# A transformer layer on one core: a new plan of the instruction order, with corrected durations and leads

## The chip, the cores and the metric

The kernel runs on 1 core of a Trainium2 chip. The metric is the time of one execution on the device in microseconds (us); it is given as the median of several runs. The engines of the core are TensorE (PE in the profile), VectorE (DVE), ScalarE (ACT), GpSimd (POOL) and SyncE (SP), which here only issues transfers. Each engine works through its own instructions in the order in which they are issued, and waits where an operand isn't there yet.

## What is computed

One layer of a transformer, in float32, for one sequence of 1024 tokens of width 1024. The mixer has sixteen groups of 64 columns from four kinds of mixing: NSA attention (compressed, selected and windowed keys with gates), a short convolution, stick-breaking attention, and dilated attention. The reference, cut to its frame:

```python
def hybrid_layer(x, ...):
    hn = rms_norm(x, g_mix)
    proj = hn @ w_in                      # split into the columns of the four mixers
    o_a = nsa_mixer(qa, ...)              # 4 heads
    o_b = short_conv_mixer(cvb, cvc, cvu, conv_w)
    o_c = stick_breaking_attention(qc, kc, vc)        # 4 heads
    # q and k of the dilated heads are normed; three dilations, mixed by a softmax over their lse
    o_d = jnp.sum(mix_w[..., None] * jnp.stack(outs, axis=0), axis=0)
    groups = rms_norm(groups, g_out.reshape(N_GROUPS, HEAD_DIM)).reshape(b, s, MIX_WIDTH)
    x = x + groups @ w_out
    h2 = rms_norm(x, g_ffn)
    return x + (jax.nn.silu(h2 @ w_gate) * (h2 @ w_up)) @ w_down      # d_ff = 2816
```

## The kernel before

**Products.** A float32 product is made as three products of a faster type on PE (`mm3`, L240 to L243): each operand is split into a high part (a copy, mostly by ACT, L107) and a low part (the difference, by POOL or DVE, L108), and high·high, high·low and low·high are summed in PSUM. Tiles are named by what they hold, with a number when they are told apart: `PRp`, `Tp`, `SPp` and `Op` are PSUM banks of four kinds, `S` scores, `pth`/`ptl` transposed probabilities in two parts, `MO` a block of the mixer's output (64 channels of two heads by 256 tokens), `whi`/`wlo` and `fw` split weights, `raw`/`fraw` weights as loaded.

**Stages.** First the input's norm, projections and the compressed keys. Then the mixers in the order `n0 c0 n1 c1 ps0 s0 ps1 s1 pd0 d0 pd1 g d1`: n are NSA heads by pairs (`attn_nsa`, L626), c the convolution (`conv`, L798), ps and pd the projections of stick-breaking and dilated heads (`proj_stick`, `proj_dil`), s and d their attention, and g the gains of the grouped norm (`gains`). Last the output projection with residual (`out_half`, L893), the second norm, and the feed-forward part: gate and up as Winograd's seven products per 2x2 of blocks (`winograd`, L1036; its additions are all at L1033), the products of down likewise. The projections of the values are transposed: ACT copies the product to `vraw` (L367), PE transposes it in four (L370), ACT and DVE split it into `VD` or `VC` (L373, L374). The dilated heads' queries and keys go through L311/L312 (`dqh`, `dql`, on 64 partitions) and L319 to L321 (`dkh`, `dkl`, `dkr`; a transfer at L320 copies each to the other 64 partitions). Outputs of a block of attention leave PSUM by an ACT copy `otmp` (L580) and a DVE add on 64 partitions (L582). `finish` (L592) norms a block: squares, a product with a block matrix of ones (L608), Ln and Exp on ACT (L609, L610), a DVE multiply, and a store of `MO` to the DRAM tile `mixd` (L617; the last one by `flush_stores`, L621). `gains` loads the seven rows of `mixd` back as `gm` (L836, 512 KB each); `gain` scales each by the norm's weight into the high part `MH` (L817 on POOL for one half of the tokens, L819 on ACT for the other) and the low part `ML` (L820, DVE). The eighth row stays in SBUF. In NSA, L549 subtracts distances and takes the minimum (`mm`) of a block of scores; L651 scales the probabilities by `ll`, L685 multiplies queries with compressed keys.

**The order.** What the program text says is not the order of issue. The program is recorded once; `_traced` (L1912) finds each instruction's dependences, gives it a duration by a formula (`_duration`, L1849) and a lead: `EARLIER` by kind plus `LEADS` by group, which is engine, pool tag and tile name, plus `LEADS` by group and stage (`@10`, the number of marks passed; 6 is s0, 10 is d0, 12 is g, 13 is d1, 15 gate/up). `_planned` (L1972) then runs a model of the five engines: of the instructions whose operands are there, each engine takes the one with the smallest number less its lead; tiles get slots when they are first written; a transfer takes a fixed time and a time for its bytes. `fix_order` (L2135) makes each engine issue in order of the planned starts, up to the first instruction that uses the pool `f2`: the products of down run in program order. The second recording gets the same slots.

## Time and profile before

| | us |
|---|---|
| median of 3 runs | 1306.11 |
| lowest, highest | 1305.69, 1307.82 |
| the profiled execution's own time | 1303.94 |
| its span, first to last instruction | 1302.1 |
| PE busy | 1276.2 |
| DVE busy | 977.5 |
| ACT busy | 701.9 |
| POOL busy | 654.5 |
| mean granted clock of PE, share of full speed | 0.997 |

All times of rows come from the one profiled execution, and count from the start of its span. An engine's busy time divided by the span says how full it is, the idle time of the fullest one where time is lost. The list of waits names, for each place where PE stood still, what released it; the timeline shows the instructions of an engine in order with their starts.

### The profile page before, as it was taken

How to read it: one execution, taken by the hardware profiler on the slowest of the kernel's cores; microseconds unless marked ns; L12 is line 12 of the kernel's file. 1: busy time of each engine (PE TensorE's matmuls, PEld its weight loads, DVE VectorE, ACT ScalarE, POOL GpSimd, SP SyncE). 2: the span in 40 equal slices, each digit the busy share in tenths (PEclk: the TensorE clock that was granted, in tenths of full speed). 3: DMA queues.
4: the chain of work that ended last, by engine and by line, in shares of the span. 5: the costliest groups of instructions: out<-in, count | busy, mean ns of one | idle time of the engine just before them, and what ended most of it. 6: DMA issues, size and time to landing. Idle time of an engine off the chain costs nothing.

```text
span 1302.1 us, 20263 instructions
## 1 busy us (share of the span) xinstructions
PE 1276.2 (98%) x7041; PEld 1086.6 (83%) x7041; DVE 977.5 (75%) x1793; ACT 701.9 (54%) x1437; POOL 654.5 (50%) x490
## 2 busy tenths in 40 slices
PE   8999999999999999999999999999999999999998
PEld 7988888888888898899987888878888787887886
DVE  5858888888898888962577788676776667499962
ACT  6567678678888877653654332332333335523540
...
GB/s 250 97 125 6 9 91 24 18 82 56 46 48 25 94 68 138 173 107 162 188 175 121 186 154 178 94 86 121 120 91 81 98 113 345 265 199 73 145 98 153
DMA packets 90550, 153.04 MB, mean 118 GB/s; under 512 B 10128, under 2 KB 35728, under 8 KB 90448
## 3 DMA queue, kind: packets, MB, share of 16 engines
...
q0 software_dynamic: 560, 1.84, 0.4%
...
q14 instruction: 47, 0.39, 0.1%
...
## 4 chain that ended last, share of the span: by engine, by line
PE 85%; DVE 7%; DMA 2%; ACT 2%; issue 2%; POOL 1%; SPq 0%; DVEq 0%; POOLq 0%; ACTq 0%
PE PRp L241 11%; PE PRp L243 10%; PE PRp L242 10%; PE Tp L570 4%; PE PRp L1056 4%; PE PRp L1054 4%; PE PRp L1055 4%; PE SPp L522 3%; PE SPp L1056 2%; PE Tp L1056 2%; PE SPp L1054 2%; PE Tp L1054 2%; PE SPp L1055 2%; PE Tp L1055 2%; PE Op L575 2%; PE SPp L524 2%
## 5 line engine op out<-in xcount | busy, mean ns | idle before, releaser
L108 POOL TENSOR_TENSOR wlo<-raw,whi 128x512 fp32r<-128x512 f32 x94 | 129.4, 1385 | 84.9 <-ACT whi L107 56.2
L1043 POOL TENSOR_TENSOR fw<-fraw,fw 128x512 fp32r<-128x512 f32 x50 | 72.5, 1449 | 131.7 <-ACT fw L1042 118.9
L559 DVE TENSOR_TENSOR ptl<-Tp,pth 128x512 fp32r<-128x512 f32 (+2 forms) x172 | 102.2, 605 | 20.2 <-ACT pth L558 17.9
L1114 DVE TENSOR_TENSOR fw<-sraw,fw 128x512 fp32r<-128x512 f32 x73 | 91.6, 1273 | 33.1 <-ACT fw L1113 32.7
L558 ACT ACTIVATE pth<-Tp 128x512 fp32r<-128x512 f32 (+2 forms) x172 | 90.3, 531 | 44.0 <-PE Tp L570 15.0
L1042 ACT ACTIVATE fw<-fs 128x512 fp32r<-128x512 f32 x88 | 52.6, 628 | 105.1 <-DVE fs L1033 77.2
L1114 POOL TENSOR_TENSOR hw<-bB,hw 128x512 fp32r<-128x512 f32 x55 | 81.0, 1486 | 47.8 <-ACT hw L1113 47.1
L570 PE MATMUL Tp<-ident,S 128*128 128x128 f32 x552 | 94.0, 275 | 1.2 <-DVE S L651 0.7
L241 PE MATMUL PRp<-XH,whi 128*128 128x512 f32 x224 | 91.3, 408 | 0.9 <-ACT raw L357 0.9
L242 PE MATMUL PRp<-XL,whi 128*128 128x512 f32 x224 | 90.3, 403 | 0.0
L243 PE MATMUL PRp<-XH,wlo 128*128 128x512 f32 x224 | 90.0, 403 | 0.0
L107 ACT ACTIVATE whi<-raw 128x512 fp32r<-128x512 f32 x102 | 63.0, 620 | 46.4 <-PE PRp L242 19.5
L1043 DVE TENSOR_TENSOR fw<-fs,fw 128x512 fp32r<-128x512 f32 x88 | 71.9, 846 | 14.8 <-ACT fw L1042 14.7
L651 POOL TENSOR_SCALAR S<-S,ll 128x640 f32<-128x640 f32 (+7 forms) x32 | 53.6, 1675 | 54.1 <-DVE ll L649 19.3
L570 PEld LDWEIGHTS Tp<-ident,S 128*128 128x128 f32 x552 | 67.7, 141 | 11.5 <-DVE ptl L559 1.4
L243 PE MATMUL PRp<-whi,ML 128*128 128x256 f32 (+1 forms) x248 | 71.0, 289 | 1.0 <-DVE ML L820 1.0
L1033 POOL TENSOR_TENSOR u<-u,p 128x512 f32<-128x512 f32 x22 | 32.2, 1462 | 78.9 <-DVE u L1033 40.8
L793 POOL TENSOR_TENSOR S<-S,R 128x128 f32<-128x128 f32 (+7 forms) x32 | 45.7, 1430 | 51.0 <-DVE R L791 49.3
L241 PE MATMUL PRp<-whi,MH 128*128 128x256 f32 (+1 forms) x248 | 70.7, 288 | 0.4 <-DVE x L903 0.4
L242 PE MATMUL PRp<-wlo,MH 128*128 128x256 f32 (+1 forms) x248 | 70.9, 287 | 0.0
L1042 ACT ACTIVATE fw<-fraw 128x512 fp32r<-128x512 f32 x50 | 31.4, 627 | 69.9 <-PE Tp L1056 18.1
L1113 ACT ACTIVATE hw<-bB 128x512 fp32r<-128x512 f32 x62 | 38.9, 628 | 53.1 <-PE Op L243 21.5
...
## 6 DMA issues: line engine op xcount, KB each, us to landing
...
```

Source lines behind the costliest of these rows:

```text
L108: (lo or nc.gpsimd).tensor_tensor(dst_lo, raw, f(dst_hi), op=OP.subtract)
L241: nc.tensor.matmul(ps, a[0], b[0], start=first, stop=False)
L242: nc.tensor.matmul(ps, a[0], b[1], start=False, stop=False)
L243: nc.tensor.matmul(ps, a[1], b[0], start=False, stop=last)
L558: nc.scalar.activation(ph[:, c], tp[:, :n], AF.Copy)
L559: nc.vector.tensor_tensor(pl[:, c], tp[:, :n], f(ph[:, c]), op=OP.subtract)
L570: nc.tensor.transpose(tp[:, i * 128:(i + 1) * 128], p, ident)
L1043: eng.tensor_tensor(wt[:, 1, :], a, f(wt[:, 0, :]), op=OP.subtract)
L1054: nc.tensor.matmul(ps, wt[:, 0, c], bh[:, k, :], start=k == 0, stop=False)
L1055: nc.tensor.matmul(ps, wt[:, 0, c], bl[:, k, :], start=False, stop=False)
L1056: nc.tensor.matmul(ps, wt[:, 1, c], bh[:, k, :], start=False, stop=k == 3)
L1114: eng.tensor_tensor(wt[:, 1, :], raw, f(wt[:, 0, :]), op=OP.subtract)
```

## The change

Three things, all in the planning; no instruction is added or taken away, and no operand changes. First, durations: narrow fp32r products on PE get a floor of 110 ns instead of 56 (times 0.92), except where the next one has the same stationary operand; ACT and DVE instructions on at most 64 partitions get 115 ns more; the constants of ACT, DVE and POOL rise by some 7 to 35 ns. Second, the table `LEADS` is new as a whole: 523 entries for 563, 356 of them for one stage (358 before). Third, `REUSES` names two more pools.

```diff
-REUSES = {"bp": ("sm",), "lp": ("sm",)}
+REUSES = {"bp": ("sm",), "lp": ("sm",), "lq": ("sm",), "b2": ("lq",)}
...
 LEADS = {
...
-    "ACT otmp tk @10": -205,
...
-    "DVE whl u": -1153,
-    "DVE whl u @15": -17,
...
+    "ACT otmp tk @10": -4858,
...
+    "DVE whl u": 3741,
+    "DVE whl u @15": -1289,
...
     if eng == "PE":
         if "float32r" in str(i.ins[1].dtype):
-            return max(56, n * 35 / 32 / 2.4) * PE_RATE
+            return max(110, n * 35 / 32 / 2.4) * PE_RATE
...
+    extra = 115 * (outs[0].ap[0][1] <= 64 and n > 1)
     if eng == "ACT":
-        return n / 1.2 + (51 if psum else 93) + 93 * small
+        return n / 1.2 + (66 if psum else 103) + 93 * small + extra
...
-            return 2.13 * n + 62 + 61 * (small > 0)
+            return 2.13 * n + 69 + 61 * (small > 0)
         if ty == "InstTensorCopy" and not psum:
-            return .52 * n + 69
+            return .52 * n + 77 + extra
         if ty == "InstTensorScalarPtr" and len(big) == 1 and not psum:
-            return .52 * n + 69 + 61 * small
-        return 1.04 * n + 69 + 61 * (max(0, small - 1) if ty == "InstCustomDveAnt" else small)
+            return .52 * n + 77 + 61 * small
+        return 1.04 * n + 78 + extra + 61 * (max(0, small - 1) if ty == "InstCustomDveAnt" else small)
     if ty == "InstDMACopy":
         return 1000
     if ty == "InstTensorScalarPtr":
-        return 2.5 * n + 260
+        return 2.5 * n + 280
...
-    return 165 * n + 300 if "pow" in str(i) else 2.1 * n + 150
+    return 165 * n + 300 if "pow" in str(i) else 2.1 * n + 185
...
-    ops, history, first, tags, bare = [], {}, {}, {}, {}
+    ops, history, first, tags, bare, last = [], {}, {}, {}, {}, None
...
+        if op.eng == "PE" and "float32r" in str(i.ins[1].dtype) and acc[0].n < 240:
+            w = str(i.ins[1].bass_ap)
+            narrow, last = (ops[last[1]] if last and last[0] == w else None), (w, op.n)
+            if narrow:
+                narrow.dur = acc[0].n * 35 / 32 / 2.4 * PE_RATE
+        elif op.eng == "PE":
+            last = None
```

Three places in the order that comes out. The first is DVE at the end of gate/up (1080 us of the profile before): `u2`, `u3` and `p5` are running sums of the seven products, PRp_12198 is the product with T4, PRp_12179 that with B22, Op_12140 that with B21, and `fw` the low parts of split weights for down. Before, DVE has:

```order
L1114 TENSOR_TENSOR fw_12250<-fraw_12248,fw_12250 128x512
L1114 TENSOR_TENSOR fw_12254<-fraw_12248,fw_12254 128x512
L1033 TENSOR_TENSOR u2_12101<-PRp_12179,u2_12101 128x512
L1114 TENSOR_TENSOR fw_12259<-fraw_12257,fw_12259 128x512
L1033 TENSOR_TENSOR u2_11960<-u2_12101,u2_11960 128x512
L1033 TENSOR_TENSOR p5_11994<-p5_12135,p5_11994 128x512
L1033 TENSOR_TENSOR u3_12156<-PRp_12198,u3_12156 128x512
L1033 TENSOR_TENSOR u3_12015<-u3_12156,u3_12015 128x512
L1033 TENSOR_TENSOR s2_12218<-s1_12216,p1_11938 128x512
L1114 TENSOR_TENSOR fw_12263<-fraw_12257,fw_12263 128x512
```

and in the changed kernel:

```order
L1114 TENSOR_TENSOR fw_12250<-fraw_12248,fw_12250 128x512
L1033 TENSOR_TENSOR u2_12101<-PRp_12179,u2_12101 128x512
L1114 TENSOR_TENSOR fw_12254<-fraw_12248,fw_12254 128x512
L1033 TENSOR_TENSOR u2_11960<-u2_12101,u2_11960 128x512
L1114 TENSOR_TENSOR fw_12259<-fraw_12257,fw_12259 128x512
L1033 TENSOR_TENSOR p5_11994<-p5_12135,p5_11994 128x512
L1033 TENSOR_TENSOR p1_12079<-Op_12140,p1_12079 128x512
L1033 TENSOR_TENSOR u3_12156<-PRp_12198,u3_12156 128x512
L1033 TENSOR_TENSOR p1_11938<-p1_12079,p1_11938 128x512
L1114 TENSOR_TENSOR fw_12263<-fraw_12257,fw_12263 128x512
L1033 TENSOR_TENSOR u3_12015<-u3_12156,u3_12015 128x512
```

The sum `p1` with the product Op_12140, which stood further ahead, now lies between `p5` and the sum with PRp_12198. On PE the product PRp_12198 stands 12 matmuls earlier, and Op_12140 is the last one; from there to the matmul that takes the bank of PRp_12198 again there are seven.

The second is DVE in the first NSA stage (160 us). S_1918 are the probabilities of one block, ll_1917 its sums; MO_1735 the output of the block before; Sc0_782 compressed scores. Before:

```order
L549 ISA S_1984,mm_1981<-SPp_1986,W_1303,mm_1981 128x256
L549 ISA mm_1981 128x1
L549 ISA S_1984,mm_1981<-SPp_1996,W_1303,mm_1981 128x256
L549 ISA mm_1981 128x1
L582 TENSOR_TENSOR MO_1735<-Op_1736,otmp_1886 64x128
L559 TENSOR_TENSOR ptl_1911<-Tp_1907,pth_1910 128x256
L582 TENSOR_TENSOR MO_1735<-Op_1736,otmp_1886 64x128
L549 ISA Sc0_782,mm_2065<-SPp_2063,wct_1306 128x63
L549 ISA mm_2065 128x1
L651 TENSOR_SCALAR S_1918<-S_1918,ll_1917 128x768
```

and in the changed kernel:

```order
L549 ISA S_1984,mm_1981<-SPp_1986,W_1303,mm_1981 128x256
L549 ISA mm_1981 128x1
L559 TENSOR_TENSOR ptl_1881<-Tp_1877,pth_1880 128x256
L549 ISA S_1984,mm_1981<-SPp_1996,W_1303,mm_1981 128x256
L549 ISA mm_1981 128x1
L549 ISA Sc0_782,mm_2065<-SPp_2063,wct_1306 128x63
L549 ISA mm_2065 128x1
L651 TENSOR_SCALAR S_1918<-S_1918,ll_1917 128x768
L582 TENSOR_TENSOR MO_1735<-Op_1736,otmp_1886 64x128
L559 TENSOR_TENSOR ptl_1911<-Tp_1907,pth_1910 128x256
```

L651 on S_1918, which the transposes on PE read, goes ahead of L582, L559 and L582.

The third is the end of attention (515 to 540 us), on ACT. gm_6885 and gm_6891 are the last two of the seven rows read back, tk_6463 the norm of the last block of d0, PRp_6906 the projection of the last pair's keys. Before, L609 and L610 on tk_6463 stand among the first five rows' L819:

```order
L819 ACTIVATE MH_6853<-gm_6855,go_119 128x512
L609 ACTIVATE tk_6463<-Tp_6465,epst_126 128x256
L819 ACTIVATE MH_6853<-gm_6861,go_119 128x512
L610 ACTIVATE tk_6463<-tk_6463 128x256
L819 ACTIVATE MH_6853<-gm_6867,go_119 128x512
L819 ACTIVATE MH_6853<-gm_6873,go_119 128x512
```

and further down, from L609 on the next block (tk_6987) to the last two L819:

```order
L609 ACTIVATE tk_6987<-Tp_6989,epst_126 128x256
L610 ACTIVATE tk_6987<-tk_6987 128x256
L751 ACTIVATE S_7107,ll_7112<-S_7107,mm_7111 128x640
L558 ACTIVATE pth_7053<-Tp_7049 128x384
L751 ACTIVATE S_7109,ll_7112<-S_7109,mm_7111 128x640
L558 ACTIVATE pth_7070<-Tp_7065 128x512
L819 ACTIVATE MH_6853<-gm_6885,go_119 128x512
L580 ACTIVATE otmp_7061<-Op_7035 64x256
L558 ACTIVATE pth_7082<-Tp_7078 128x384
L819 ACTIVATE MH_6853<-gm_6891,go_119 128x512
```

In the changed kernel ACT has:

```order
L605 ACTIVATE pth_6466<-tk_6463 128x256
L311 ACTIVATE dql_6477<-PRp_6897,gsc_118 64x512
L319 ACTIVATE dkh_6478<-PRp_6906,gsc_118 64x512
L819 ACTIVATE MH_6853<-gm_6885,go_119 128x512
L609 ACTIVATE tk_6463<-Tp_6465,epst_126 128x256
L610 ACTIVATE tk_6463<-tk_6463 128x256
L319 ACTIVATE dkl_6479<-PRp_6906,gsc_118 64x512
L751 ACTIVATE S_7107,ll_7112<-S_7107,mm_7111 128x640
L558 ACTIVATE pth_6960<-Tp_6956 128x384
L819 ACTIVATE MH_6853<-gm_6891,go_119 128x512
```

The L819 on gm_6885 now stands directly ahead of L609 on tk_6463. On SP, the store that comes of that block (L621) and the last loads stand as follows before:

```order
L621 DMA mixd_75<-MO_6352 128x256
L536 DMA zq_4194<-dqh_6476 64x128
L536 DMA zq_4196<-dqh_6476 64x128
L320 DMA dkh_6478<-dkh_6478 64x512
L131 DMA raw_7779<-in_wout_dram 128x2x256
L536 DMA zq_4194<-dql_6477 64x128
L536 DMA zq_4196<-dql_6477 64x128
L320 DMA dkl_6479<-dkl_6479 64x512
L536 DMA zq_4194<-dqh_6476 64x128
L836 DMA gm_6885<-mixd_75 128x1024
L536 DMA zq_4194<-dql_6477 64x128
L836 DMA gm_6891<-mixd_75 128x1024
```

and in the changed kernel:

```order
L536 DMA zq_4196<-dql_6477 64x128
L836 DMA gm_6885<-mixd_75 128x1024
L536 DMA zq_4196<-dqh_6476 64x128
L536 DMA zq_4194<-dqh_6476 64x128
L536 DMA zq_4196<-dql_6477 64x128
L536 DMA zq_4194<-dql_6477 64x128
L320 DMA dkh_6478<-dkh_6478 64x512
L621 DMA mixd_75<-MO_6352 128x256
L320 DMA dkl_6479<-dkl_6479 64x512
L131 DMA raw_7779<-in_wout_dram 128x2x256
L536 DMA zq_4194<-dqh_6476 64x128
L836 DMA gm_6891<-mixd_75 128x1024
```

The load of gm_6885 goes ahead of the store L621 by six places, where it was nine behind it. On PE there are 58 rows between the L608 of tk_6463 and the first product with gm_6891's row in the changed kernel, and work of some 23 us before.

## Rows read from the trace of the kernel before

**Rows 1.** The page's shares of the engines (busy time, share of the span, number of instructions), and its chain of waits, by engine.

```profile
PE 1276.2 (98%) x7041; PEld 1086.6 (83%) x7041; DVE 977.5 (75%) x1793; ACT 701.9 (54%) x1437; POOL 654.5 (50%) x490
...
PE 85%; DVE 7%; DMA 2%; ACT 2%; issue 2%; POOL 1%; SPq 0%; DVEq 0%; POOLq 0%; ACTq 0%
```

**Rows 2.** The table by stretches: the stretch in us and its length; busy time of PE, of PE's weight loads, DVE, ACT and POOL with the number of instructions; PE's granted clock (a share of 2.4 GHz); the share of the DMA engines; GB/s.

```profile
0.00:14.00 14.00, 8.69 (x48) 7.86 (x49) 5.47 (x15) 6.78 (x11) 5.28 (x15) 0.96 0.83 292
100.00:570.00 470.00, 458.74 (x2983) 404.60 (x2984) 400.94 (x1035) 362.75 (x805) 224.18 (x171) 1.00 0.22 66
157.00:163.00 6.00, 4.59 (x25) 3.10 (x23) 5.66 (x18) 4.92 (x12) 3.84 (x3) 0.99 0.00 0
163.00:167.00 4.00, 3.92 (x16) 3.43 (x17) 2.49 (x11) 1.96 (x5) 3.81 (x3) 0.58 0.00 0
550.00:600.00 50.00, 49.69 (x415) 48.99 (x414) 25.45 (x51) 24.53 (x49) 16.72 (x14) 1.00 0.42 132
600.00:650.00 50.00, 50.00 (x382) 47.89 (x381) 24.70 (x48) 26.85 (x60) 36.38 (x32) 1.00 0.51 168
1074.00:1084.00 10.00, 8.42 (x36) 6.52 (x36) 6.50 (x11) 3.27 (x6) 5.21 (x5) 1.00 0.88 304
```

**Rows 3.** What PE waited for, over the whole span: engine, tile and line that waited, what released it; us in total, times, the longest.

```profile
PE PRp L370 <- ACT vraw L367: 2.0, 4, 0.9
...
PE PRp L241 <- DVE u L1033: 1.6, 1, 1.6
...
PE Tp L570 <- DVE S L651: 0.7, 1, 0.7
...
PE SPp L522 <- DMA dkl<-dkl: 0.6, 1, 0.6
...
PE SPp L685 <- DVE mm L549: 0.4, 1, 0.4
```

**Rows 4.** The timeline of DVE from 520 to 525.5, in a projection of the dilated stage: start, duration, instruction; in brackets the idle time before it and what ended it. Rows of one engine can overlap, so the distance of two starts is what one instruction costs the next.

```profile
521.79 0.74 DVE L312 SCALAR_TENSOR_TENSOR dqh<-PRp,gsc,dqh 64x512 fp32r<-64x512 f32 x1
522.56 0.74 DVE L321 SCALAR_TENSOR_TENSOR dkr<-PRp,gsc,dkh 64x512 fp32r<-64x512 f32 x1
523.34 0.42 DVE L582 TENSOR_TENSOR MO<-Op,otmp 64x256 f32<-64x256 f32 x1
523.79 0.76 DVE L312 SCALAR_TENSOR_TENSOR dql<-PRp,gsc,dql 64x512 fp32r<-64x512 f32 x1
```

**Rows 5.** The timeline of PE, 1081 to 1084.5, the end of gate/up.

```profile
1082.77 0.50 PE L241 MATMUL PRp<-fw 128*128 128x512 f32 x1 [1.58 <-DVE u L1033]
1083.11 0.39 PE L242 MATMUL PRp<-fw 128*128 128x512 f32 x1
1083.34 0.40 PE L243 MATMUL PRp<-fw 128*128 128x512 f32 x1
```

**Rows 6.** The timeline of DVE at the same place.

```profile
1079.55 0.69 DVE L1033 TENSOR_TENSOR u<-u,u 128x512 f32<-128x512 f32 x1 [1.19 <-POOL u L1033]
1081.42 0.69 DVE L1033 TENSOR_TENSOR p<-p,p 128x512 f32<-128x512 f32 x1 [1.18 <-POOL p L1033]
1082.03 0.68 DVE L1033 TENSOR_TENSOR u<-PRp,u 128x512 f32<-128x512 f32 x1
```

**Rows 7.** The timeline of POOL at the same place.

```profile
1077.90 1.61 POOL L1033 TENSOR_TENSOR u<-u,p 128x512 f32<-128x512 f32 x1 [3.96 <-ACT fw L1113]
1079.59 1.80 POOL L1033 TENSOR_TENSOR p<-u,p 128x512 f32<-128x512 f32 x1
```

**Rows 8.** The timeline of DVE from 155 to 168, in the first NSA stage.

```profile
160.26 0.28 DVE L582 TENSOR_TENSOR MO<-Op,otmp 64x128 f32<-64x128 f32 x1
160.55 0.42 DVE L559 TENSOR_TENSOR ptl<-Tp,pth 128x256 fp32r<-128x256 f32 x1
160.99 0.28 DVE L582 TENSOR_TENSOR MO<-Op,otmp 64x128 f32<-64x128 f32 x1
...
161.45 1.58 DVE L651 TENSOR_SCALAR S<-S,ll 128x768 f32<-128x768 f32 x1
```

**Rows 9.** Issued transfers by tile: queue, number, KB each, median us from the issue to the landing.

```profile
mixd<-MO SPq DMA_DIRECT2D x20, 128.0 KB, 1.9
...
dkl<-dkl SPq DMA_DIRECT2D x4, 128.0 KB, 2.6
```

**Rows 10.** The timeline of PE from 529 to 538.5, the start of the output projection.

```profile
537.79 0.39 PE L243 MATMUL PRp<-whi,ML 128*128 128x256 f32 x1 [1.04 <-DVE ML L820]
538.01 0.28 PE L241 MATMUL PRp<-whi,MH 128*128 128x256 f32 x1
538.13 0.28 PE L242 MATMUL PRp<-wlo,MH 128*128 128x256 f32 x1
```

**Rows 11.** The timeline of ACT from 515 to 540, the end of attention.

```profile
528.83 0.47 ACT L609 ACTIVATE tk<-Tp,epst 128x256 f32<-128x256 f32 x1 [2.18 <-PE Tp L608]
529.34 0.42 ACT L610 ACTIVATE tk<-tk 128x256 f32<-128x256 f32 x1
...
533.87 0.71 ACT L819 ACTIVATE MH<-gm,go 128x512 fp32r<-128x512 f32 x1
```

**Rows 12.** All that touches the tile gm: the last line, its seven loads' time from issue to landing.

```profile
DMA to landing us min/median/max: 3.5/5.0/8.9
```

More of the change, by code (lines that the diff above doesn't have):

```diff
@@ L1801 @@
-    "SP whl p": 1857,
-    "SP whl p @15": -231,
+    "ACT B22 B": -2264,
+    "ACT B22 B @14": -2099,
+    "ACT QK St": 538,
+    "ACT QK St @0": -2302,
+    "ACT QK ckh": 1567,
+    "ACT QK ckh @5": 2749,
+    "ACT QK ckh @7": 633,
+    "ACT QK ckl": -1090,
+    "ACT QK ckl @7": -29,
+    "ACT QK cqh": 287,
+    "ACT QK cqh @5": -11178,
+    "ACT QK cqh @7": -1400,
+    "ACT QK cql": 1642,
+    "ACT QK cql @5": 734,
+    "ACT QK cql @7": 2386,
+    "ACT QK dkh": -4102,
+    "ACT QK dkh @10": 147,
@@ new lines @@
+    "ACT QK dkh @11": 1603,
+    "ACT QK dkh @13": -9064,
+    "ACT QK dkh @9": 77,
+    "ACT QK dkl": 1065,
+    "ACT QK dkl @10": 6,
+    "ACT QK dkl @13": 435,
+    "ACT QK dkl @9": 363,
+    "ACT QK dqh": -1424,
+    "ACT QK dqh @10": 2462,
+    "ACT QK dqh @13": 209,
+    "ACT QK dqh @9": -5,
+    "ACT QK dql": 909,
+    "ACT QK dql @10": 391,
+    "ACT QK dql @11": -4066,
+    "ACT QK dql @13": -1417,
+    "ACT QK dql @9": -2,
+    "ACT QK er": 5038,
+    "ACT QK er @14": 1276,
+    "ACT QK fw": -1255,
@@ new lines @@
+    "ACT S4 cm": -3182,
+    "ACT S4 cm @0": 162,
+    "ACT S4 kv": 4108,
+    "ACT S4 kv @0": 2136,
+    "ACT S4 wa": 1814,
+    "ACT S4 wa @0": -1725,
+    "ACT T3 T": 128,
+    "ACT T3 T @14": -4745,
+    "ACT T4 T": -5167,
+    "ACT T4 T @14": -10,
+    "ACT V VA": -1375,
+    "ACT V VA @0": 1772,
+    "ACT V VC": 506,
+    "ACT V VC @5": 106,
+    "ACT V VC @7": 2332,
+    "ACT V VD": -6,
+    "ACT V VD @11": -4449,
+    "ACT V VD @9": 108,
+    "ACT V bhl": -289,
+    "ACT V bhl @0": 1045,
@@ new lines @@
+    "ACT tk sq @11": -3063,
+    "ACT tk sq @9": -1191,
+    "ACT tk vraw": -140,
+    "ACT tk vraw @5": -7699,
+    "ACT tk vraw @7": 1900,
+    "ACT tk vraw @9": -23,
+    "ACT vcHL vcHL": -942,
+    "ACT vcHL vcHL @0": -848,
+    "ACT whl c @15": -2751,
+    "ACT whl p": -4819,
+    "ACT whl p @15": 592,
+    "ACT whl sh": 766,
+    "ACT whl sh @2": -73,
+    "ACT whl sh @4": 1387,
+    "ACT whl u": -171,
+    "ACT whl u @15": -1202,
+    "ACT whl whi": -580,
+    "ACT whl whi @0": 1151,
+    "ACT whl whi @11": -33,
@@ new lines @@
+    "ACT whl whi @14": 882,
+    "ACT whl whi @2": -3097,
+    "ACT whl whi @4": 3132,
+    "ACT whl whi @5": 7369,
+    "ACT whl whi @7": -1534,
+    "ACT whl whi @9": 611,
+    "DVE B22 B @14": -3927,
+    "DVE MO MO": -488,
+    "DVE MO MO @1": 188,
+    "DVE MO MO @10": 9889,
+    "DVE MO MO @13": -1737,
+    "DVE MO MO @3": 887,
+    "DVE MO MO @8": -336,
+    "DVE QK St": 70,
+    "DVE QK St @0": -453,
+    "DVE QK ckr": -1400,
+    "DVE QK ckr @5": 2379,
+    "DVE QK ckr @7": -7380,
+    "DVE QK cqh": -218,
@@ new lines @@
+    "DVE df fs": 331,
+    "DVE df fs @15": 1683,
+    "DVE epst epst": -1417,
+    "DVE gates gates": -1741,
+    "DVE gates gates @0": -2115,
+    "DVE gsc gsc": 1473,
+    "DVE gsc gsc @0": -1613,
+    "DVE gt gt @0": 3623,
+    "DVE half half": -1904,
+    "DVE half half @0": -1749,
+    "DVE hss hss": -5255,
+    "DVE hss hss @0": 2,
+    "DVE hss hss @11": -3509,
+    "DVE hss hss @9": -1053,
+    "DVE ident ident": -1393,
+    "DVE ident ident @0": -634,
+    "DVE kcTl kcTl": 10,
+    "DVE kcTl kcTl @0": 143,
@@ new lines @@
+    "DVE ll ll": -30,
+    "DVE ll ll @1": 7135,
+    "DVE ll ll @10": -1368,
+    "DVE ll ll @13": -965,
+    "DVE ll ll @3": -1616,
+    "DVE mm mm": -283,
+    "DVE mm mm @1": -436,
+    "DVE mm mm @10": -4060,
+    "DVE mm mm @13": -1713,
+    "DVE mm mm @3": 79,
+    "DVE nt nt": 1223,
+    "DVE nt nt @14": 6249,
+    "DVE one1 one": 6827,
+    "DVE one1 one @0": -4509,
+    "DVE pad0 Sc @1": 2806,
+    "DVE pad0 Sc @3": 3332,
+    "DVE pad1 Sc": -1187,
+    "DVE pad1 Sc @1": -142,
+    "DVE pad1 Sc @3": -4,
@@ new lines @@
+    "POOL whl wlo @9": -2368,
+    "SP QK ckh": 2417,
+    "SP QK ckh @5": 171,
+    "SP QK ckh @7": -1015,
+    "SP QK ckl": 1608,
+    "SP QK ckl @5": 242,
+    "SP QK ckl @7": -1576,
+    "SP QK dkh": 76,
+    "SP QK dkh @10": -649,
+    "SP QK dkh @11": 5205,
+    "SP QK dkh @13": 2524,
+    "SP QK dkh @9": -1026,
+    "SP QK dkl": 1024,
+    "SP QK dkl @11": 861,
+    "SP QK dkl @13": 3510,
+    "SP QK dkl @9": 1193,
+    "SP QK fraw": -13,
+    "SP QK fraw @14": -231,
+    "SP QK fraw @15": -5430,
```

924 lines of the change are left out of this document (368 added, 556 removed).

## The prediction

> **What bounds the kernel now.** I read the engines' shares and the chain of waits first: TensorE (PE) is busy 1276.2 of 1302.1 us, and the chain that ended last runs through PE for 85% of the span and through VectorE (DVE) for 7% [rows 1]. The change alters no instruction, only the order in which each engine issues them and the slots that tiles take, so PE's work is fixed, and all that can be won is its idle time, 1302.1 - 1276.2 = 25.9 us, and time at a lower clock. Then the table by stretches, to see where the idle time lies: 11.26 us (470 - 458.74) in the attention stages from 100 to 570, 5.31 in the first 14, 1.58 in 1074 to 1084; from 600 to 650 PE is busy 50.00 of 50.00 [rows 2]. In 100 to 570 DVE is busy 400.94 of 470, from 550 on only 25.45 and 24.70 of 50 [rows 2]: attention leans on DVE, and there an order planned with wrong DVE durations can hurt. Then PE's list of waits, which says what was late at each stall [rows 3], and the timeline around three of them.
>
> **The corrected durations.** Are they nearer to the trace? DVE's 64x512 with a scalar starts 0.77 and 0.78 us ahead of the next instruction, the 64x256 add 0.45 [rows 4]; the old formulas give 0.662 and 0.335, the new ones 0.787 and 0.459 (mine, from the lines of the diff). They are, and the old plan was short on DVE by about 0.12 us for each such instruction. That alone moves nothing on the chip: an engine starts when its operands are there, whatever the plan thought. The two entries added to REUSES name pools that the kernel doesn't have, and cost and bring nothing. What counts is the order that comes out, with a new table of leads besides, so I went through the places.
>
> **End of gate/up, 1080 us: -1.6.** PE stands 1.58 us before a product that takes over a PSUM bank [rows 5]. DVE's add that empties the bank (start 1082.03) stood behind an add on p, which DVE could start only at 1081.42 since it waited for GpSimd (POOL): u 1.61 us, p 1.80 us [rows 6, 7]. In the new order the product in that bank stands 12 matmuls earlier and B21's product last, so POOL's chain (1.61 + 1.80, and about 1.6 for the DVE adds and hand-overs on either side, 5.0 in all) runs under 24 matmuls of 0.23 us [rows 5], 5.6 us. After the last product DVE has two adds (0.61 each from start to start [rows 6], and 0.3 to hand over: 1.5 us) and PE seven matmuls (1.6 us) before it needs the bank. Cover by 0.1: I take the whole stall as gone; at worst it stays (0).
>
> **The stall at 160: -2.5.** PE idles 1.41 in 157 to 163, waits 0.7 of it for DVE's S (L651) and 0.4 for mm, and just behind that, in 163 to 167, the granted clock is 0.58 [rows 2, 3], about the lower level of 1.2 GHz: 3.92 us busy at 0.58 are 2.27 of work, 1.65 lost. In the new order L651 stands ahead of two L582 and one L559, which lay from 160.26 to 161.45 [rows 8]: it can start 1.19 sooner, more than the 0.7, and the minimum of the next scores (L549) goes ahead of them too (the 0.4). That is 1.1 of the idle time, and of the 1.65 I take 1.4, as 0.3 of the idle time may stay in front of it. At most -3.1, at worst 0 (the stall moves to the L582 that is now later).
>
> **dkl: -0.6.** PE waited 0.6 for the transfer of dkl [rows 3], which stood behind five gm loads of 512 KB on SP's queue; it now stands ahead of them. It is 128 KB and lands in 2.6 by the median [rows 9]: -0.6, at worst 0.
>
> **Transposes of V: +0.5.** PE waits 2.0 for vraw in 4 places [rows 3]. The new order puts some of these transposes right behind the projection product whose copy they need, where rows of other work lay between; two others, in the last dilated stage, are now covered. A bare one costs up to 0.9, the longest of the four. Two or three newly bare, two newly covered: from +0.2 to +1.2, I take +0.5.
>
> **The rest of the small waits: -3.1.** Of the 11.26 idle in 100 to 570 I have named 1.41, 2.0 (vraw), 0.6 (dkl) and 1.04 (below) [rows 2, 3, 10]. There remain 6.2 in waits of a few tenths for DVE and ScalarE (ACT). Where an order puts an instruction that PE waits for behind one that nobody waits for, truer durations take that out; where DVE is just full, no order does. The trace of before doesn't tell the two apart. Bounds: -6.2 and, with the same waits elsewhere and half as many again, +3. I take half of the gain.
>
> **End of attention: +2.2.** The output projection's products need the mixed rows read back from DRAM (gm), scaled into MH (L819, ACT) and ML (L820, DVE). Before, PE lost 1.04 here, to ML [rows 10]. The path of the last block of the first dilated half: L609 0.47, L610 0.42, a DVE multiply of about 0.42, the store's 1.9 to land, the load's 3.5 to 5.0, L819 0.71, 0.2 to hand over [rows 9, 11, 12]: 7.6 to 9.1 us. In the new order ACT has L819 on gm_6885 directly ahead of that L609 (before, L609 stood 27 rows ahead), and PE has only 58 matmuls between the block's sum (L608) and the first product that needs the row, most of them 256 wide at 0.12 [rows 10], 6.6 us in all; before it had 23 us of work there. So PE waits 1.0 to 2.5; I take 1.8. The row before that is late as well: gm_6885's load waits on SP's queue for a slot that an L820 frees, and ACT's L819 for the load; 0 to 3.4, I take 1.4. Less the 1.04 of before: +2.2, from 0 to +4.9.
>
> What is queued behind these waits: on ACT, L609 and so the block's store; on SP, that store itself, six places behind gm_6885's load. The rows show SP's wait only through its end, the landing. The Trainium skill ("DMA: Bandwidth & Descriptors", section "Anatomy of one DMA — SWDGE (gpsimd) path") states that a transfer's wait for a semaphore is spent on the sequencer that issues it, before dispatch, which speaks against this piece of the change: the store can't pass the load. The same section puts a transfer at 2.0 us and bytes/436e3 us: an estimate from the page of 2.3 for the store and 3.2 for the load, 5.5 together, where the rows have 5.4 to 6.9; by the page the sum would be about 0.7 us lower.
>
> **Start:** the 5.31 idle us of the first 14 stay, since the first rows of every engine are as they were: 0. The W-down part isn't planned at all: 0.
>
> **Sum:** -1.6 - 2.5 - 0.6 + 0.5 - 3.1 + 2.2 = -5.1. The profiled execution took 1303.94 (span 1302.1 and 1.84 around it): 1298.8. The median of the runs is 1306.11, 2.17 above it; with the same offset, **1301.0**. A difference under 0.2% (2.6 us) can't be told from none here.
>
> **Rivals.**
> Same, 1304.1: DVE is late in attention because it has too much to do, 400.94 of 470, and another order only moves the small waits. For it: PE, DVE and ACT are all at their fullest there. Against: DVE has 69 us to spare in that stretch, and PE is short by only 2.4% [rows 2]. Then the -3.1 falls away: -2.0. With the V transposes and the end of attention at their upper ends as well (+1.2, +4.9) it is +1.4, 1307.5, still the same. Chance 0.25.
>
> Slower, 1310.4: the load of the last gm row decides. Landings go from 3.5 to 8.9 [rows 12], and this one runs beside other gm loads, weights of the output projection and rows of x. At 8.9 PE waits 9.1 + 3.9 - 6.6 = 6.4 for it and 1.4 for the row before, less 1.04: +6.8; a stall of that length may lower the clock as the one at 160 did, +1.7 [rows 2]. With none of the small waits won: -1.6 - 2.5 - 0.6 + 0.5 + 8.5 = +4.3. The point of decision: with the small waits at 0, the end of attention must cost over 4.2, that is a load over some 6.3 us before any loss of clock; with them at -3.1, over 7.3. For it: ACT and SP work in order, and the longest transfer of the stage lies on PE's path. Against: the median landing is 5.0. Chance 0.23.
>
> More than forecast, 1294.8: all of the small waits go (-6.2), the load lands in 3.5 (0 for the end of attention), the clock stays up (-3.1) and the V transposes cost 0.2: -11.3. It is the far end of the forecast's own case, as DVE has room for it.
>
> **How the numbers follow.** Faster 0.52, same 0.25, slower 0.23. The forecast's own range goes from 1294.8 to 1303.5; below 1296.0, where every bound has to fall on the good side, I leave out some 7 in 100. Upward the range takes in all of the case of no difference (to 1308.7) and the nearer part of the slower one, to 1309.5; some 13 in 100 lie beyond.
>
> **What would show it.** PE's busy time some 1274.5 (1276.2 less what the clock gave back) and its idle time about 22. At the end of gate/up no wait of PRp for u; at 160 no clock of 0.58 and no wait for S; dkl gone from the list of waits; vraw at 2.5; waits for MH or ML of 2.5 to 4 us ahead of the output projection; the rest of the idle time in 100 to 570 about 3.1 instead of 6.2. The forecast is wrong if the clock falls in a new place (1.7 each), if the end of attention costs over 5, or if DVE's adds at 1080 still come late because POOL starts later than the B22 product.

## The result and the profile after

| | before | after |
|---|---|---|
| median of the runs, us | 1305.90 (1305.31 to 1307.82, 4 runs) | 1298.93 (1297.82 to 1299.60, 4 runs) |
| profiled execution, own time | 1303.94 | 1299.38 |
| its span | 1302.1 | 1297.6 |

The ratio of the times is 0.9943, with a 95% interval from 0.9926 to 0.9960: faster by 0.57%, 7.0 us between the medians. The two profiled executions lie only 4.56 us apart, since that of before was 2 us under its median and that of after 0.45 over; a second measurement further down gives 0.9939. So the traces below show places, and the medians the size.

The page of after, engines and chain of waits [rows 1]:

```profile
PE 1273.9 (98%) x7041; PEld 1087.2 (84%) x7041; DVE 973.4 (75%) x1793; ACT 700.5 (54%) x1437; POOL 644.9 (50%) x490
...
PE 88%; DVE 4%; DMA 3%; ACT 2%; issue 1%; POOL 0%; SPq 0%; ACTq 0%; DVEq 0%
```

TensorE is 23.7 us idle (1297.6 - 1273.9) where it was 25.9; the chain has more of PE and less of DVE (4% for 7%). The table by stretches, columns as in [rows 2]:

```profile
0.00:14.00 14.00, 9.41 (x58) 8.54 (x59) 5.34 (x16) 7.50 (x13) 6.51 (x16) 1.00 0.83 321
80.00:90.00 10.00, 9.09 (x50) 8.46 (x51) 6.07 (x11) 5.97 (x15) 5.44 (x5) 0.66 0.30 102
100.00:570.00 470.00, 459.05 (x3008) 407.75 (x3008) 393.86 (x1023) 359.13 (x798) 221.69 (x174) 1.00 0.22 65
157.00:163.00 6.00, 6.00 (x42) 5.33 (x41) 5.73 (x24) 5.70 (x13) 5.58 (x4) 1.00 0.00 0
163.00:167.00 4.00, 4.00 (x30) 3.71 (x29) 3.94 (x13) 3.94 (x10) 3.48 (x3) 1.00 0.31 78
1074.00:1084.00 10.00, 10.00 (x45) 8.06 (x44) 9.57 (x12) 5.09 (x9) 7.61 (x10) 1.00 0.97 344
```

Two places of before are clean: 157 to 163 and 1074 to 1084 are full, and 163 to 167 is at full clock. The first 14 us hold 9.41 busy for 8.69. Between 100 and 570 PE is still idle 10.95 us, where it was 11.26. And there is a new stretch at a granted clock of 0.66, from 80 to 90.

What PE waited for [rows 3]:

```profile
PE PRp L370 <- ACT vraw L367: 2.2, 4, 0.7
...
PE SPp L522 <- DVE mm L549: 2.0, 5, 0.6
PE Op L576 <- DVE ptl L559: 1.7, 2, 1.5
PE PRp L241 <- DVE VD L374: 1.2, 2, 0.8
...
PE SPp L522 <- DMA dkh<-dkh: 0.3, 1, 0.3
PE PRp L243 <- DVE ML L820: 0.3, 1, 0.3
...
PE PRp L241 <- ACT MH L819: 0.2, 1, 0.2
```

The waits for u, for S and for dkl are gone; those for vraw are as long as before (2.2 for 2.0); ML, MH and dkh are small. In their place stand small waits for mm, a wait of 1.5 for ptl and two for VD.

### The profile page after: what moved, and what is told of

The parts are those of the page before. It is cut to its first block, busy times and chain, and to the rows that moved or that the text cites. A ratio compares the mean times of both kernels' runs of the same rounds, so it can differ in the third digit from the quotient of the medians.

```text
span 1297.6 us, 20242 instructions
## 1 busy us (share of the span) xinstructions
PE 1273.9 (98%) x7041; PEld 1087.2 (84%) x7041; DVE 973.4 (75%) x1793; ACT 700.5 (54%) x1437; POOL 644.9 (50%) x490
## 3 DMA queue, kind: packets, MB, share of 16 engines
q0 software_dynamic: 560, 1.84, 0.3%
## 4 chain that ended last, share of the span: by engine, by line
PE 88%; DVE 4%; DMA 3%; ACT 2%; issue 1%; POOL 0%; SPq 0%; ACTq 0%; DVEq 0%
PE PRp L241 11%; PE PRp L243 11%; PE PRp L242 11%; PE Tp L570 4%; PE PRp L1054 4%; PE PRp L1055 4%; PE PRp L1056 4%; PE SPp L522 2%; PE SPp L1054 2%; PE Tp L1054 2%; PE SPp L1055 2%; PE Tp L1056 2%; PE SPp L1056 2%; PE Tp L1055 2%; PE Op L575 2%; PE Op L576 2%
## 5 line engine op out<-in xcount | busy, mean ns | idle before, releaser
L108 POOL TENSOR_TENSOR wlo<-raw,whi 128x512 fp32r<-128x512 f32 x94 | 126.9, 1357 | 81.3 <-ACT whi L107 61.5
L559 DVE TENSOR_TENSOR ptl<-Tp,pth 128x512 fp32r<-128x512 f32 (+2 forms) x172 | 101.6, 604 | 27.6 <-ACT pth L558 25.2
L241 PE MATMUL PRp<-XH,whi 128*128 128x512 f32 x224 | 91.0, 406 | 0.0
L570 PE MATMUL Tp<-ident,S 128*128 128x128 f32 x552 | 86.4, 274 | 0.7 <-DVE ptl L559 0.4
L651 POOL TENSOR_SCALAR S<-S,ll 128x640 f32<-128x640 f32 (+7 forms) x32 | 53.7, 1677 | 62.1 <-DVE ll L649 20.7
L570 PEld LDWEIGHTS Tp<-ident,S 128*128 128x128 f32 x552 | 65.4, 140 | 9.0 <-DVE ptl L559 1.6
L241 PE MATMUL PRp<-whi,MH 128*128 128x256 f32 (+1 forms) x248 | 71.5, 290 | 1.4 <-DVE VD L374 0.8
L1033 DVE TENSOR_TENSOR fs<-fraw 128x512 f32<-128x512 f32 x44 | 41.7, 948 | 35.8 <-DMA fraw<-in_wgate_dram 20.2
L793 POOL TENSOR_TENSOR S<-S,R 128x128 f32<-128x128 f32 (+7 forms) x32 | 46.9, 1466 | 35.9 <-DVE R L791 30.7
```

Of the source, the lines that this page charges most:

```text
L108: (lo or nc.gpsimd).tensor_tensor(dst_lo, raw, f(dst_hi), op=OP.subtract)
L241: nc.tensor.matmul(ps, a[0], b[0], start=first, stop=False)
L559: nc.vector.tensor_tensor(pl[:, c], tp[:, :n], f(ph[:, c]), op=OP.subtract)
L570: nc.tensor.transpose(tp[:, i * 128:(i + 1) * 128], p, ident)
```

## The experiments

All times are medians; each ratio is that to runs of the kernel before on the same chip, with its 95% interval. Theory A says that a few places made the gain, by what stands first there; theory B, that truer durations made a better order all through attention; theory C, which came up after the first four, that an order is as good as the leads chosen for just that set of durations, and that any disturbance draws another one.

**Half of the change, or one stage of it.** Here the kernel holds both tables and both sets of formulas; two sets of stages say where the new ones hold. With all stages in both it gives the order of the changed kernel, with none the order of before.

```diff
-        op.dur, op.port = _duration(i, op.eng, acc), _port(i, op.eng, acc)
+        st = sum(m <= op.n for m in marks)
+        op.dur = (_duration_new if st in NEW_TIMES else _duration_old)(i, op.eng, acc)
+        op.port = _port(i, op.eng, acc)
...
-            op.lead += LEADS.get(op.group, 0) + LEADS.get(op.stage, 0)
+            table = LEADS_NEW if st in NEW_LEADS else LEADS_OLD
+            op.lead += table.get(op.group, 0) + table.get(op.stage, 0)
```

leads_only (all stages in NEW_LEADS, none in NEW_TIMES), expected:

> The new table of leads with the old durations, everywhere. Theory A (the gain is made at a few places, by which instruction stands first there; the durations only set what the leads must be): the leads carry the order, so most of the gain stays, some 3 to 7 us under before. Theory B (the gain comes from truer durations throughout attention): with the old durations the new leads are mismatched, same as before or up to 3 us over it, and PE's idle time in 100 to 570 rises above 11 us.

times_only (none in NEW_LEADS, all in NEW_TIMES), expected:

> The new durations with the old table of leads, everywhere. Theory A: the old leads were matched to the old durations, so the places move at random; 0 to 5 us over before. Theory B: truer durations alone take small waits out, 3 to 6 us under before, PE's idle time in 100 to 570 at 8 us or less.

ff_only (stage 15, gate/up, in both), expected:

> New durations and leads for the gate/up stage alone, all else by the old ones. Theory A: the stall of 1.58 us at the end of gate/up goes and nothing else changes, 1.6 us under before (some 0.12%). Theory B: durations there are those of 128 partitions, which changed by under 10 ns, no gain: within 0.5 us of before.

nsa_only (stages 1 to 4 in both), expected:

> New durations and leads for NSA and convolution alone (the stages n0, c0, n1, c1). Theory A: the stall at 160 and the half clock behind it go, the rest stays as it falls out: 2 to 3 us under before, and the stall of 1.6 at the end of gate/up stands. Theory B: the small waits between 170 and 310 go as well, 4 us or more under before.

| kernel | us | ratio | PE idle in 100 to 570 |
|---|---|---|---|
| leads_only | 1317.93 | 1.0095 (1.0075 to 1.0114) | 470 - 454.54 = 15.46 |
| times_only | 1322.69 | 1.0134 (1.0114 to 1.0154) | 470 - 449.39 = 20.61 |
| ff_only | 1303.26 | 0.9979 (0.9966 to 0.9992) | 470 - 458.10 = 11.90 |
| nsa_only | 1321.71 | 1.0123 (1.0100 to 1.0146) | 470 - 449.66 = 20.34 |

Each half of the change alone is slower than both whole kernels, by 12 to 24 us. Both theories missed both of these: A had leads_only 3 to 7 us faster and times_only at most 5 slower, B had leads_only at most 3 slower and times_only 3 to 6 faster. nsa_only, which was to be 2 us faster or more by either, lost 16: PE's idle time rises by 1.45 us in 100 to 310, its own stages, and by 7.6 in 310 to 570 behind them. Most of the other 7 is clock: the mean granted clock of its six runs is 0.9918, that of the 17 runs of before beside them 0.9968, and the difference on 1300 us is 6.5 us (an estimate from the two means). I take it that a moved NSA hands the later stages another situation than their leads were chosen for. Only ff_only did what theory A expected, and a reason is at hand, though not tested by itself: nothing that is planned comes behind that stage. Its PE was busy 30.00 of 30 in 1070 to 1100, the stall at the end of gate/up gone; the 500 matmuls around that place, from the 6001st on, take it 1.79 us less than before (116.45 for 118.24), while the runs say 2.7, with 1.0 to 4.4 in the interval.

**Does the order come from truer durations?** The table of leads empty, with the old and with the new formulas:

```diff
 LEADS = {
-    "ACT B22 B": -1620,
...
 }
```

Expected of zero_old:

> The old durations with an empty table of leads. To be compared with zero_new. Theory B (truer durations make a better order by themselves): well over zero_new, by 5 us or more. Theory C (an order is as good as the leads that were chosen for just these durations; durations alone move it at random): within 5 us of zero_new on either side; in both theories 20 us or more over before.

Expected of zero_new:

> The new durations with an empty table of leads. Theory B: 5 us or more under zero_old. Theory C: within 5 us of it on either side, and 20 us or more over the changed kernel.

zero_old took 1331.64 us (1.0195, 1.0169 to 1.0222), zero_new 1336.50 (1.0232, 1.0205 to 1.0259). Truer durations alone made the order no better; it was 4.9 us worse, just inside what C allows, and one pair can't say more than that. Without its leads before loses some 25 us, the changed kernel some 38.

**How far a good order stands by itself.** One constant of the planner in the changed kernel, by one nanosecond:

```diff
-        return 1.04 * n + 78 + extra + 61 * (max(0, small - 1) if ty == "InstCustomDveAnt" else small)
+        return 1.04 * n + 79 + extra + 61 * (max(0, small - 1) if ty == "InstCustomDveAnt" else small)
```

> The changed kernel with one constant of the planner changed by 1 ns: 79 instead of 78 for VectorE's general instructions. Theory C (leads fit one order; any disturbance draws another order at random): 5 to 20 us over the changed kernel. Theory B (the order is good because the durations are true): 1 ns is no worse a duration, within 2 us of it.

It took 1319.08 us (1.0099, 1.0073 to 1.0125), 21 us over the changed kernel in the same measurement, and PE stood idle 470 - 445.83 = 24.2 us in 100 to 570. No duration is truer or less true by 1 ns; theory B is out. C holds in the main, with a loss a little above its 20. But leads that don't fit their durations are still worth something: leads_only stands at 1.0095 where zero_old, with the same durations, has 1.0195, and times_only and a_1ns at 1.0134 and 1.0099 where zero_new has 1.0232.

**Five instructions by hand at 160 us.** From here on the plan is taken as it is, and only named instructions are put elsewhere in the order of their engine, so that no other row moves.

```diff
+MOVED = ((1399, 1435), (1416, 1435), (1400, 1435), (1417, 1440), (1418, 1440))
...
     program = _program(tc)
+    start = list(start)
+    for k, (n, behind) in enumerate(MOVED):
+        start[n] = start[behind] + 1e-6 * (k + 1)
```

Numbers 1399, 1416 and 1400 are the two L582 and the L559, 1435 is L651, 1417 and 1418 are L694 and L695, 1440 is the last of the four transposes.

> The plan of before with five instructions moved by hand at 160 us and nothing else: on VectorE L651 ahead of L582, L559, L582, and on TensorE the two products that need these (L694, L695) behind the transposes that need L651. Theory D (place on VectorE): L651 starts about 1 us sooner and takes 1.58 as before; TensorE's wait for S goes, 0.7 to 1.1 us less idle time, and the half clock at 163 to 167 may go (1.65 more): 1 to 2.8 us under before. Theory P (it waits for GpSimd, which ran S of its own to 161.3 and two L607 after it, wherever it stands): it ends when GpSimd's instruction ends; if it gets in between GpSimd's two instructions it ends near 161.9 and the gain is that of D, if not it ends at 163.0 again, with a duration of over 2.5 us and no gain.

DVE in b160, then POOL in b160 and POOL in before, then the stretches of b160:

```profile
160.48 0.61 DVE L651 TENSOR_SCALAR S<-S,ll 128x768 f32<-128x768 f32 x1
161.13 0.28 DVE L582 TENSOR_TENSOR MO<-Op,otmp 64x128 f32<-64x128 f32 x1
```

```profile
159.29 2.49 POOL L651 TENSOR_SCALAR S<-S,ll 128x768 f32<-128x768 f32 x1 [9.63 <-DVE ll L649]
```

```profile
161.33 1.28 POOL L607 TENSOR_TENSOR sl<-yc,sh 128x512 fp32r<-128x512 f32 x1
```

```profile
157.00:163.00 6.00, 5.01 (x28) 3.71 (x28) 5.66 (x23) 5.43 (x15) 3.71 (x3) 1.00 0.00 0
163.00:167.00 4.00, 4.00 (x29) 3.53 (x28) 3.70 (x11) 3.48 (x7) 3.81 (x4) 1.00 0.01 2
```

L651 starts 0.97 us sooner than in [rows 8] and takes 0.61 instead of 1.58, while POOL's own L651 runs from 159.29 to 161.78. So the place on DVE decides, as theory D has it, though D had expected the 1.58 to stay; and for POOL's L651 theory P falls, as this instruction didn't wait for that one. For POOL's next instruction P fits. In before DVE's L651 starts at 161.45, 0.12 us after POOL's first L607 (161.33 to 162.61), and ends at 163.03, 0.42 after it; in ff_only, with the same order here, it starts 0.12 after L607 and ends 0.42 after it again. In b160 L651 ends 1.94 us sooner, one half by its place and one half, it seems, because it stands ahead of that L607. The wait for S is gone and so is the half clock, though PE is still idle 0.99 in 157 to 163, 0.42 of it less than before. In the trace the NSA stages end 1.05 us sooner. The runs give 1305.14 us, 0.9993 (0.9980 to 1.0006): 0.9 us, not clear of nothing.

**Two small transfers at the start.** The prediction left out SP's first instructions. Before, then after:

```profile
0.73 0.38 SPq L217 DMA_DIRECT2D bgt<-in_bgate_dram  x1
1.17 0.42 SPq L428 DMA_DIRECT2D pet<-in_pe_dram  x1
1.64 0.42 SPq L208 DMA_DIRECT2D xt<-in_x_dram  x1
```

```profile
0.73 0.38 SPq L208 DMA_DIRECT2D xt<-in_x_dram  x1
```

The first load of x goes out 0.91 us sooner, since the transfers of bgt and pet are no longer ahead of it. On before, with these two alone moved behind the eight loads of x:

```diff
+MOVED = ((54, 53), (215, 53))
```

> The plan of before with two small transfers moved on SyncE's queue and nothing else: bgt and pet, which are issued first, behind the eight loads of the input's rows. Theory S (they hold the first load of x, and with it ScalarE's first instruction, up): ScalarE starts at 4.6 instead of 5.4, the first weight products some 1 us sooner, and where the clock doesn't fall at 13 us another 1.6: 0.8 to 2.4 us under before. Rival (the loads share the DMA engines anyway, the wait moves to the split of the first weights): the wait for whi grows by what xn gains, same as before.

ACT's first instruction on x in b_start:

```profile
4.59 1.06 ACT L174 ACTIVATE xn<-xt 128x1024 f32<-128x1024 f32 x1 [2.58 <-DMA xt<-in_x_dram]
```

It starts at 4.59, in before at 5.42 and in after at 4.63. The last transpose of x starts 1.84 us sooner than before (41.74 for 43.58), partly because the clock stayed up at 13 us. The profiled execution as a whole is no shorter (1302.3 for 1302.1), although it has one stretch of half clock, in 80 to 90, where before has two, in 10 to 20 and 163 to 167: at its 2500th matmul it is 0.6 us ahead of before, at its last one 0.2 behind. So this trace shows the start and not the gain. The runs say 1303.55 us, 0.9978 (0.9969 to 0.9988): 2.9 us for two transfers of a few KB. Theory S has the place right, and its rival falls, as the wait for whi went down too, from 1.5 to 1.0; but S allowed 2.4 at most. Part of the gain is clock all over the kernel: the mean granted clock of these eleven runs is 0.9980, that of the 17 of before beside them 0.9966, and the difference on 1300 us is 1.8 us (an estimate from the two means). Why the clock falls less often with this start is not shown.

**The changed kernel once more.**

> The changed kernel unchanged, to see whether the half clock at 81 to 88 us is part of the order or of the single execution. If of the order: the granted clock is below 1 there again, for 6 us. If of the execution: shorter, longer or absent, and the span 1.5 to 3.5 us off 1297.6. The time 1298 to 1300.

1297.87 us, 0.9939 (0.9922 to 0.9957). The stretches from 10 to 20 and from 80 to 90 in the table by stretches, first of before, then of ff_only, whose order is that of before up to gate/up, then of after_again:

```profile
10.00:20.00 10.00, 7.87 (x48) 7.50 (x49) 6.09 (x10) 7.54 (x14) 7.08 (x6) 0.83 1.03 404
80.00:90.00 10.00, 8.03 (x65) 7.35 (x64) 4.96 (x10) 6.77 (x17) 7.49 (x6) 1.00 0.42 123
```

```profile
10.00:20.00 10.00, 7.70 (x39) 7.50 (x40) 5.52 (x9) 6.54 (x14) 6.76 (x6) 0.66 1.03 404
80.00:90.00 10.00, 7.97 (x39) 6.93 (x39) 5.65 (x11) 6.32 (x15) 6.73 (x5) 0.67 0.39 120
```

```profile
10.00:20.00 10.00, 8.89 (x58) 8.41 (x59) 5.62 (x10) 7.54 (x14) 7.75 (x7) 0.83 1.00 372
80.00:90.00 10.00, 8.45 (x69) 7.77 (x68) 6.35 (x12) 6.95 (x16) 6.77 (x6) 1.00 0.30 87
```

The same order on every engine in these stretches, and the granted clock is 0.83 and 1.00 in one execution, 0.66 and 0.67 in another. The changed kernel had 1.00 and 0.66 in the first profile and 0.83 and 1.00 in this one. So the half clock at 80 to 90 is not the new order's; where it falls belongs to the single execution, and it is one reason why runs of one kernel lie 2 to 9 us apart: of the 17 runs of before beside leads_only the fastest, 1302.44, has a mean granted clock of 0.999, and the slowest, 1311.11, 0.993. How much of it there is does differ between the orders: the six runs here have 0.9985 on the mean (the four of the first measurement 0.9975), the 17 of before beside them 0.9966. Of the 8 us between the two (0.61% of 1306.8) that makes some 2.4, by the same estimate as for b_start.

The trace of after_again also tells where the rest was won. PE is ahead of before by 0.9 us at its 500th matmul, 3.7 at the 2500th, 3.4 at the 4000th and 6.1 at the last one (counts, and so only nearly the same places, as the orders differ): at the start, by 160 us and in gate/up, and nothing in the rest of attention.

**One instruction at 438 us.** In after, between 434 and 443:

```profile
438.17 2.37 POOL L793 TENSOR_TENSOR S<-S,R 128x1024 f32<-128x1024 f32 x1
438.28 0.60 ACT L558 ACTIVATE pth<-Tp 128x512 fp32r<-128x512 f32 x1 [0.42 <-PE Tp L570]
438.50 2.33 DVE L611 TENSOR_TENSOR MO<-MO,tk 128x256 f32<-128x256 f32 x1
...
440.75 0.68 DVE L559 TENSOR_TENSOR ptl<-Tp,pth 128x512 fp32r<-128x512 f32 x1
...
441.48 0.39 PE L576 MATMUL Op<-ptl,VC 128*128 128x256 f32 x1 [1.46 <-DVE ptl L559]
```

PE waits 1.46 for ptl (L559), which stands on DVE behind L611. L611 takes 2.33 us (the median of its 24 in this trace is 0.425), and it ends 0.29 us after POOL's L793, which runs to 440.54. It isn't alone: all six of the 24 that take over 0.5 us end 0.28 or 0.29 us after a TENSOR_TENSOR of POOL that had begun before them, twice L793 and four times L108. In a438 L611 alone is moved behind L559 and the next L549:

```diff
+MOVED = ((3926, 4536),)
```

> The changed kernel with one instruction moved: VectorE's L611 at 438.5 us behind the copy ptl (L559) and the next L549. Theory P (L611 took 2.33 us instead of 0.42 because GpSimd's L793 ran from 438.17 to 440.54): ptl runs at once, TensorE's wait of 1.46 us for it goes, L611 stands behind until 440.5 or takes 0.42: 1.4 us under the changed kernel, 1297.5. Rival (something else held VectorE): ptl itself takes over 2 us there, the wait stays, no gain.

DVE in a438:

```profile
436.61 0.69 DVE L559 TENSOR_TENSOR ptl<-Tp,pth 128x512 fp32r<-128x512 f32 x1 [0.33 <-ACT pth L558]
...
437.43 2.56 DVE L611 TENSOR_TENSOR MO<-MO,tk 128x256 f32<-128x256 f32 x2
439.90 1.28 DVE L559 TENSOR_TENSOR ptl<-Tp,pth 128x512 fp32r<-128x512 f32 x2
```

L559 runs at once; the two L611 that now stand together take 2.56 where nobody waits for them, and end 0.29 us after L793 (438.26) and 0.28 after the L108 behind it (439.70). So theory P holds and its rival falls. PE's wait is gone, and in the trace PE gains 1.1 us on the changed kernel between its 2500th and its 3000th matmul. 1.4 us of another wait appear at 496, for the load of W: from the 2500th to the 3500th matmul it takes 146.9 us, where after took 146.5 and after_again 147.8. The runs: 1296.46 us, 0.9925 (0.9909 to 0.9941). That is the lowest median of all, but its interval overlaps those of the changed kernel, so a gain is not shown.

**Eleven instructions by hand.** The two bare groups of transposes and the two at 513 us as well:

```diff
+MOVED = ((3926, 4536), (3731, 3739), (3732, 3739), (3733, 3739), (3734, 3739),
+         (4473, 4481), (4474, 4481), (4475, 4481), (4476, 4481), (4887, 5214), (4888, 5215))
```

> The changed kernel with eleven instructions moved by hand: VectorE's L611 at 438 us as in a438 (-1.1 to -1.4), the bare transposes of V at 362 and 423 us behind the next three projection products (-0.57 and -0.75, their waits), and at 513 us L373 on ScalarE ahead of L580 and L374 on VectorE ahead of L582 (-0.4 of 0.8). If waits taken out early stay out: 2 to 2.8 us under the changed kernel. If they come back at the next thing that is late (the load of W at 494 us, the end of attention): 1 or less.

Waits of PE in a_best from 345 to 410, then from 410 to 480:

```profile
PE Tp L570 <- ACT tk L609: 0.9, 1, 0.9
PE Tp L570 <- DVE ptl L559: 0.7, 1, 0.7
PE Tp L570 <- ACT S L794: 0.2, 1, 0.2
```

```profile
PE PRp L241 <- ACT vraw L367: 0.7, 1, 0.7
PE PRp L370 <- ACT vraw L367: 0.7, 1, 0.7
```

1299.67 us, 0.9947 (0.9931 to 0.9963): nothing gained, though its profiled execution had no half clock at all:

```profile
10.00:20.00 10.00, 8.37 (x62) 7.70 (x63) 6.60 (x12) 7.98 (x16) 8.57 (x8) 1.00 0.99 371
80.00:90.00 10.00, 8.97 (x73) 8.50 (x74) 7.17 (x13) 6.93 (x17) 6.80 (x5) 1.00 0.32 102
```

At 362 the transposes of V were covered, and 0.57 us of waiting became 1.8: the L570 behind them needs a bank that ACT's L609 empties, and comes too early now. At 423 the wait only changed its name: the next product (L241) uses the bank that the same ACT copy empties. Two moves that looked free in the list of waits had a second resource behind them.

## Why the prediction was right, and where not

The time, -5.1 against 1306.11 forecast, was 1298.93, inside the range; and the likeliest case came, at 1.4 times its size. By its own steps:

- **End of gate/up, -1.6: right.** PE is full there in after, the 500 matmuls around the place take 1.78 us less than before, and ff_only gets the same alone.
- **The stall at 160, -2.5: right.** 1.41 idle and 1.65 of clock are gone at that place (in this execution some 3.1 of clock were lost in 80 to 90 instead, 9.09 busy at 0.66; in after_again not). The step on L651 held as well. Here is the L549 on the last block of scores ahead of it, first before, then after, and after's L651:

```profile
159.73 0.48 DVE L549 CUSTOM_DVE_ANT_0 S<-SPp,W,mm 128x256 f32<-128x256 f32 x1
```

```profile
161.02 0.48 DVE L549 CUSTOM_DVE_ANT_0 S<-SPp,W,mm 128x256 f32<-128x256 f32 x1
...
161.56 1.02 DVE L651 TENSOR_SCALAR S<-S,ll 128x768 f32<-128x768 f32 x1
```

  L651 stands 0.54 us behind that L549, where it stood 1.72 behind it: 1.18 sooner, for 1.19 forecast. From the start of the span it is no sooner (161.56 for 161.45) only because this execution had been late since the half clock at 80 to 90; in after_again it starts at 159.74. Not forecast was that it also takes less, 1.02 for 1.58, and that PE's order has two projection products in front of the transposes. That L651's place on DVE alone counts is told by the trace of b160, which gets 1.05; the runs of b160 don't show it clear of nothing.
- **dkl, -0.6: half.** The wait went, a wait of 0.3 for dkh came. The product with dkl at 526.8 now stands for 0.5 us for which the profile names no releaser.
- **Transposes of V, +0.5: right in sign,** 2.0 to 2.2.
- **The rest of the small waits, -3.1: wrong.** 10.95 idle in 100 to 570, less vraw 2.2, dkh 0.3, ML and MH 0.5, leaves 7.95 where 6.2 were: +1.7 (+1.3 by the trace of after_again). The term rested on truer durations making a better order. They don't: by zero_new, times_only and a_1ns an order is good only for leads and durations together. In after_again the whole stretch is idle 11.18, in before 11.26. So attention as a whole won nothing but the place at 160, and lost as much in small waits. The rival of no difference had this mechanism, but not the other terms.
- **End of attention, +2.2: wrong.** It costs 0.5 in after (ML 0.3, MH 0.2) and 1.2 in after_again (0.3 and 0.9), where it cost 1.04: -0.5 to +0.2. On PE, on ACT, on DVE and on POOL in after:

```profile
519.43 0.28 PE L608 MATMUL Tp<-ptl,blk1r 128*128 128x256 f32 x1
...
529.54 0.39 PE L241 MATMUL PRp<-whi,MH 128*128 128x256 f32 x1 [0.21 <-ACT MH L819]
```

```profile
519.22 0.71 ACT L819 ACTIVATE MH<-gm,go 128x512 fp32r<-128x512 f32 x1
519.83 0.46 ACT L609 ACTIVATE tk<-Tp,epst 128x256 f32<-128x256 f32 x1
...
528.76 0.72 ACT L819 ACTIVATE MH<-gm,go 128x512 fp32r<-128x512 f32 x1 [0.55 <-DMA gm<-mixd]
```

```profile
520.77 1.34 DVE L611 TENSOR_TENSOR MO<-MO,tk 128x256 f32<-128x256 f32 x1
```

```profile
520.55 1.28 POOL L108 TENSOR_TENSOR wlo<-raw,whi 128x512 fp32r<-128x512 f32 x1
```

  From the block's L608 to the first product that needs the last row PE has 10.1 us, of which 1.2 are waits, so 8.9 of work, not the 6.6 that I worked out: the cover was mis-sized. The path came out a little over my upper end of 9.1: from L609 at 519.83 to L819 at 528.76 and PE at 529.54 it takes 9.7. One of its steps was mis-sized too, DVE's multiply L611 with 1.34 for 0.42, as it ends 0.28 us after POOL's L108 here as well. And ACT's L819 on gm_6885, which I feared as a block ahead of L609, started at 519.22 with the load already there. The rule of the Trainium skill that I weighed, that a transfer's wait is spent on the sequencer that issues it ("DMA: Bandwidth & Descriptors", section "Anatomy of one DMA — SWDGE (gpsimd) path"), did no harm here: in after gm_6885's load went out at 515.31, and the store at 522.14, when L611 had ended. The estimate that I took from the same section, 2.3 for the store and 3.2 for the load, rests on a fit that the section states for transfers by GpSimd; on SP's queue they took 1.7 and 4.5 from issue to landing (1.7 and 5.2 in after_again).
- **Start, 0: wrong.** I read that the first rows of every engine were as they were, and they are on ACT and PE, but not on SP, whose first two rows changed. b_start gives 2.9 us for these alone (1.6 to 4.1 in the interval), some 1.8 of it clock.

What the three places give alone, ff_only, b160 and b_start, multiplies to 0.9979 x 0.9993 x 0.9978 = 0.9950, where the whole change measured 0.9943 and 0.9939. Within their intervals, over 1 us on either side for each, the three can account for the whole gain; b160 by itself is not clear of nothing, and a remainder of some 1 us means nothing at this noise. So it was luck that the total came near, as the errors cancelled: attention's small waits came out some 4.8 us worse than forecast, the end of attention 2.0 to 2.7 and the start 2.9 better. The clock was in the forecast for 1.4, at 160 alone; the runs of after_again gave back some 2.4 over the whole kernel.

What stays open: why DVE's L651 passed POOL's L651 in b160, when in after it ended 0.41 us after the same one (159.96 to 162.17) and in before 0.42 after L607; spans on POOL are rough, too. That POOL holds L611 up is told by the six cases in the trace of after and the two in a438, all of which end at the same distance from POOL's instruction; POOL's instruction itself was not moved.
